# Pooling and convolution inputs of a two-layer encoder trunk: weights stationary, channels on the partitions, straight into the padded rows

## The chip, the cores and the metric

The kernel runs on one core of a Trainium2 chip. The metric is the device time of one execution in microseconds (us), here the median of three runs. The profile shows one further execution, recorded by the hardware profiler. Engines: PE is TensorE (PEld its weight load, which runs beside the matmuls), DVE is VectorE, ACT is ScalarE, POOL is GpSimd, SP is the queue that issues the DMAs of the weights.

## The reference, cut to what matters

The trunk has two layers over x of 256 tokens and 1024 channels, all in float32. Half of a layer:

```
h = rmsnorm(x, g_pre_mix)
(c_q, c_kv, k_r, p_in, s_u, s_v, cv_b, cv_c, cv_x, gate_logits) = split_cols(h @ w_in)
        # 256, 128, 32, 256, 256, 256, 256, 256, 256 and 4 x 1024 columns
y_a = mla_branch(c_q, c_kv, k_r, ...) @ w_br_a     # 8-head latent attention, rotary key
y_b = pool_branch(p_in, ...) @ w_br_b              # trailing-window means over 2, 4, 8, 16 tokens
y_c = sgu_branch(s_u, s_v, ...) @ w_br_c           # spatial gate within blocks of 128 tokens
y_d = (cv_b * conv3(cv_c * cv_x)) @ w_br_d         # causal 3-tap convolution along the tokens
merged = sum over branches of sigmoid(gate) * y
x = x + rmsnorm(merged @ w_out, g_post_mix)
```

The other half is a SwiGLU FFN of 2816 channels between two more norms. Pooling and convolution run along the tokens, so the kernel wants their inputs p_in, cv_b and cv_c * cv_x with channels on the partitions and tokens along the row.

## The kernel before

**Products.** Float32 products are made of float32r parts. Each operand is split into a high part and the rest: `mac` (L317, L318, L319) issues three matmuls, high x high, low x high, high x low. The activations of the first norm stand as `hh` (high) and `hl` (low), one pair of tiles for each half of 128 tokens (`hT_tiles`), channels on the partitions. The gain g is multiplied in there; the reciprocal root of each token (`rstd`, one number per token) is multiplied in later, on the product.

**Weights** come in pieces of 128 x 1024 (512 KB), in the order of a plan. The SP queue brings a piece into one of four staging buffers `st`; ACT copies it rounded into the high tile (L267), DVE subtracts to get the low one (L287); both are `u` tiles, of which there are 24. `pump` starts a piece, `settle` issues the DVE half, and the staging buffer is free when the DVE half is done. A piece of the projection has 2 of the 8 blocks k of 128 rows, and all columns of its group: `unit` runs the 2 x 3 matmuls of one piece for one half, and the four pieces of a group are added up in one bank of PSUM for each half.

**Groups of the combined projection.** A is c_q, c_kv, k_r (416 columns), S the spatial gate's (512), P is p_in with cv_b, the first 256 columns of the convolution (512), C the other two (512). After them come the four branches' gates (`group2`, evicted by a tanh on ACT), two groups of 512 columns each. In every one the activations of a half are the stationary side (128 x 128), the weights move, and the result has tokens on the partitions.

- `evict_p` (ACT, L931) and `evict_c` (ACT L935, DVE L936) multiply by `rstd`, C's second half with its first in one step.
- `g_misc`, once it starts, transposes these results: per half 2 transposes of the product cv_c * cv_x, and 4 of p_in and cv_b (L439, in `transposes`), copied by ACT (L789, L794, L795) into `zT`, `pT_` and `cT_`, rows of 16 zeros and 256 tokens. Then come the convolution (L804 on ACT, L805 to L807 on DVE), the pooling, the spatial gate.

**Order.** The order on each engine is written by hand. The main line issues the units; between them `tick()` advances the spawned generators, each with a delay in ticks, then issues the waiting DVE halves of conversions, and starts the next piece when few are ahead. An engine runs its instructions in the order in which they were issued. `att` is spawned ahead of the P group with a delay of 8 ticks: `g_proj` takes sums of squares on ACT, the rotary key (`rope`, DVE, L631 and on), the reciprocal root (`g_rsqrt`, DVE, L406 to L418, one Newton step per tick), the copies of the transposed key (L664), the transposes of c_q and c_kv with their split (`split_scaled`, ACT L446, DVE L447), and then the q products. A q product is 12 matmuls of 256 columns into one of the two `mm` banks, emptied on DVE by a multiply with the table of cosines (L685), so that the third product needs the bank that the first multiply has read. `misc` (`g_misc`) is spawned behind the C group with a delay of 3. The first piece of layer 0 is converted in the prologue, and the sums of squares for `rstd` there (`g_first`) run beside the A and S groups; `finish(first)` ends them within the P group, and `g_evict` then empties the A and S banks (L889, L895).

**The FFN** has a form of product that the change uses too. `block` (L1096, L1101) takes a piece with all 8 blocks k of 128 columns. The weights are stationary; the activations move, with the high and low parts of both halves beside each other in one row of 512: 8 matmuls of high weights x 512 columns, 8 of low weights x the 256 high columns. The result has channels on the partitions; its high and low sums are added up by `total` (ACT copy L1106, DVE add L1107, DVE multiply by a row L1108). That row, `rrow`, holds the reciprocal root of each token along the row on all partitions: `g_rrow` makes it with two copies on DVE (L1085), two transposes, and a copy on ACT.

Of the kernel before, what the change touches and what calls it, by code (L numbers as in the profile page):

```python
# [11 lines left out]
F32R = mybir.dt.float32r  # L12
# [31 lines left out]
EV = 2  # L44
# [151 lines left out]
def trunk(ctx: ExitStack, tc, x, xT, wall, small, const, qtab, gpost, out):  # L196
# [156 lines left out]

    def hT_tiles(h):
        return T([P, NK, P], f"hh{h}", 1, F32R), T([P, NK, P], f"hl{h}", 1, F32R)
# [253 lines left out]
    class Part:  # L609


        def __init__(self, tiles, s, h):
            self.tiles, self.s, self.h = tiles, s, h

        def __getitem__(self, at):
            k = at[1]
            return self.tiles[k // 2][:, k % 2, self.s, self.h * P:(self.h + 1) * P]

    for l in range(NL):
        sg = gains(l)  # L620
        a_sb, s_sb, p_sb, z_sb = [None, None], [None, None], [None, None], [None, None]
# [156 lines left out]
        def g_misc():  # L778
            L = PAD + SEQ
            zT = tok()[:, :].rearrange("p (c t) -> p c t", c=2)  # L780
            cT_ = tok()[:, :].rearrange("p (c t) -> p c t", c=2)
            pT_ = tok()[:, :].rearrange("p (c t) -> p c t", c=2)
            nc.gpsimd.memset(pT_[:, :, 0:PAD], 0.0)
            nc.gpsimd.memset(zT[:, :, 0:PAD], 0.0)
# [131 lines left out]
        else:  # L916
            o = {}
            for h, i in lead_order(8):
                if h == 1 and i == 0:
                    finish(turn)  # L920
                g, w, ev = (("A", 416, evict_a), ("S", 512, evict_s))[i // 4]
# [7 lines left out]
        def evict_p(h):  # L929
            p_sb[h] = tok()  # L930
            nc.scalar.activation(p_sb[h][:, :512], pp[h], AF.Identity, scale=rstd[h])  # L931

        def evict_c(h):
            z_sb[h] = tok()
            nc.scalar.activation(z_sb[h][:, :256], pc[h][:, 0:256], AF.Identity, scale=rstd[h])  # L935
            nc.vector.scalar_tensor_tensor(z_sb[h][:, 256:512], pc[h][:, 256:512], rstd[h], z_sb[h][:, 0:256],  # L936
                                           op0=ALU.mult, op1=ALU.mult)

# [3 lines left out]
        pp = [mm(), mm()] if l == 0 else [acc(), acc()]  # L942
        if l == 0:
# [8 lines left out]
            for n, (h, i) in enumerate(pairs(4)):  # L952
                unit(l, ("P",), i, h, hT, pp[h], 512)
                if n == EV:
                    finish(first)
                    late = spawn(g_evict())
                if i == 3:
                    if h == 0:
                        finish(late)
                    evict_p(h)  # L960
# [18 lines left out]
        def g_merged(h, q):  # L979
            if q == 0:  # L980
# [4 lines left out]
            split_scaled(hh[:, 4 * q:4 * q + 4, :].rearrange("p k t -> p (k t)"),  # L985
                         hl[:, 4 * q:4 * q + 4, :].rearrange("p k t -> p (k t)"), t, 0.5)
# [94 lines left out]
        def g_rrow():  # L1081

            rb = tok()
            for h in range(2):
                nc.vector.tensor_copy(rb[:, h * P:(h + 1) * P], rf[h].to_broadcast([P, P]))  # L1085
            yield RW
            t = tp()
            transposes(t, [rb[:, h * P:(h + 1) * P] for h in range(2)])
            nc.scalar.copy(rrow, t[:, :SEQ])

        def block(key):

            pc_ = W((l,) + key)
            o = mm()
            for k in range(NK):
                nc.tensor.matmul(o, pc_[0][:, k * P:(k + 1) * P], hx[k // 2][:, k % 2].rearrange("p s t -> p (s t)"),  # L1096
                                 start=(k == 0), stop=False)
                if k == 5:
                    tick()
            for k in range(NK):  # L1100
                nc.tensor.matmul(o[:, :SEQ], pc_[1][:, k * P:(k + 1) * P], hx[k // 2][:, k % 2, 0, :], start=False,  # L1101
                                 stop=(k == NK - 1))
            return o
# [39 lines left out]
        for h, u in lead_order(8):  # L1143
            if u == 0:
                finish(gturn[h])
                if h == 1:
                    rr = spawn(g_rrow(), 1)
# [81 lines left out]
```

## Time and profile before

| what | value |
|---|---|
| three runs | 803.78, 804.70, 804.86 us; median 804.7 |
| profiled execution | 803.72 us, of which its span is 801.9 |
| mean granted clock of TensorE | 0.997 |
| matmuls of `mac` with `hh` and `hl` (L317, L318, L319) | 424 of each, 399, 387 and 388 ns |
| conversions: ACT (L267), DVE (L287) | 268 of each, mean 1047 and 1215 ns |
| busiest of DVE's and ACT's groups | L287 with 318.8 us, L267 with 273.3 us |
| transfers | 148.11 MB, mean 185 GB/s |

The span is the time from the first recorded instruction to the last. Busy time of PE counts the matmuls as their ends are modelled; a matmul's own duration is longer than the distance from its start to the next one's, since they are pipelined. In rows of instructions the columns are the start in us, the duration, the engine, the line of the kernel, the operation, output <- inputs by the program's names with their partitions x elements, and how many stand in the row; in brackets follows the idle time of the engine ahead of it, and what it waited for. In rows of the chain they are the start, the duration, the engine, output and line.

### The profile page before, as it was taken

How to read it: one execution, taken by the hardware profiler on the slowest of the kernel's cores; microseconds unless marked ns; L12 is line 12 of the kernel's file. 1: busy time of each engine (PE TensorE's matmuls, PEld its weight loads, DVE VectorE, ACT ScalarE, POOL GpSimd, SP SyncE). 2: the span in 40 equal slices, each digit the busy share in tenths (PEclk: the TensorE clock that was granted, in tenths of full speed). 3: DMA queues.
4: the chain of work that ended last, by engine and by line, in shares of the span. 5: the costliest groups of instructions: out<-in, count | busy, mean ns of one | idle time of the engine just before them, and what ended most of it. 6: DMA issues, size and time to landing. Idle time of an engine off the chain costs nothing.

```text
span 801.9 us, 10903 instructions
## 1 busy us (share of the span) xinstructions
PE 791.0 (99%) x3982; PEld 664.2 (83%) x3982; DVE 598.5 (75%) x1094; ACT 452.8 (56%) x776; POOL 3.9 (0%) x16
## 2 busy tenths in 40 slices
PE   8999999999999999999999999999999999999996
PEld 7888887888888888888788888878888888888885
DVE  6687976748888777777885698764689787777773
ACT  6767655444665555555665675644357555555551
POOL 0000000000000000000000000000000000000000
PEclk9999999999999999999999999999999999999998
DMA  8866444455564555655655545355555555655631
GB/s 305 315 218 208 159 158 157 167 207 171 191 211 152 178 196 183 201 194 171 228 158 189 209 160 179 131 175 197 181 182 186 182 184 184 192 192 187 190 106 52
DMA packets 42245, 148.11 MB, mean 185 GB/s; under 512 B 4688, under 2 KB 5840, under 8 KB 42192
## 3 DMA queue, kind: packets, MB, share of 16 engines
q1 hardware_dynamic: 41328, 145.12, 54.1%
q0 software_dynamic: 576, 2.10, 0.7%
q8 instruction: 31, 0.51, 0.3%
q10 hardware_dynamic: 288, 0.21, 0.1%
q14 instruction: 22, 0.18, 0.1%
HBM read 146.36 MB, written 1.05 MB: 184 GB/s over the span
## 4 chain that ended last, share of the span: by engine, by line
PE 86%; DVE 7%; DMA 3%; ACT 2%; issue 1%; SPq 0%; DVEq 0%; ACTq 0%
PE acc L319 18%; PE acc L317 18%; PE acc L318 18%; PE mm L1096 14%; PE mm L1101 7%; DVE u L287 3%; PE tp L439 3%; DMA st<-wall 2%; PE mm L317 2%; PE mm L318 2%; PE mm L319 2%; PE mm L714 1%; DMA x<-x 1%; PE acc L742 1%; ACT u L267 1%
## 5 line engine op out<-in xcount | busy, mean ns | idle before, releaser
L287 DVE TENSOR_TENSOR u<-st,u 128x1024 fp32r<-128x1024 f32 (+1 forms) x268 | 318.8, 1215 | 51.9 <-ACT u L267 51.5
L267 ACT ACTIVATE u<-st 128x1024 fp32r<-128x1024 f32 (+1 forms) x268 | 273.3, 1047 | 19.1 <-DMA st<-wall 18.3
L317 PE MATMUL acc<-u,hh 128*128 128x512 f32 (+1 forms) x424 | 169.1, 399 | 0.0
L319 PE MATMUL acc<-u,hh 128*128 128x512 f32 (+1 forms) x424 | 164.7, 388 | 0.2 <-DVE u L287 0.2
L318 PE MATMUL acc<-u,hl 128*128 128x512 f32 (+1 forms) x424 | 164.3, 387 | 0.0
L1096 PE MATMUL mm<-u,u 128*128 128x512 f32 x576 | 144.4, 392 | 0.0
L1096 PEld LDWEIGHTS mm<-u,u 128*128 128x128 f32 x576 | 105.3, 188 | 20.8
L317 PE MATMUL acc<-u,s2k 128*128 128x512 f32 x256 | 101.2, 395 | 0.0
L319 PE MATMUL acc<-u,s2k 128*128 128x512 f32 x256 | 100.8, 394 | 0.3 <-DVE u L287 0.3
L318 PE MATMUL acc<-u,s2k 128*128 128x512 f32 x256 | 100.4, 392 | 0.0
L319 PEld LDWEIGHTS acc<-u,hh 128*128 128x128 f32 x424 | 79.6, 188 | 17.1 <-DVE u L287 0.8
L317 PEld LDWEIGHTS acc<-u,hh 128*128 128x128 f32 x424 | 79.8, 188 | 14.4 <-issue 0.3
L318 PEld LDWEIGHTS acc<-u,hl 128*128 128x128 f32 x424 | 79.8, 188 | 14.2
L1101 PEld LDWEIGHTS mm<-u,u 128*128 128x128 f32 x576 | 78.6, 190 | 5.6
L1101 PE MATMUL mm<-u,u 128*128 128x256 f32 x576 | 80.3, 282 | 0.0
L1024 ACT ACTIVATE gate<-acc,rhalf 128x512 f32<-128x512 f32 x32 | 22.1, 689 | 64.7 <-PE acc L319 64.6
L319 PEld LDWEIGHTS acc<-u,s2k 128*128 128x128 f32 x256 | 48.1, 188 | 11.1 <-DVE u L287 1.2
L317 PEld LDWEIGHTS acc<-u,s2k 128*128 128x128 f32 x256 | 48.2, 188 | 9.3 <-issue 0.3
L318 PEld LDWEIGHTS acc<-u,s2k 128*128 128x128 f32 x256 | 48.1, 188 | 9.1
L1107 DVE TENSOR_TENSOR tok<-mm,tok 128x256 f32<-128x256 f32 x72 | 30.3, 421 | 27.6 <-ACT tok L1106 27.4
L1106 ACT COPY tok<-mm 128x256 f32<-128x256 f32 x72 | 26.6, 370 | 42.6 <-PE mm L1101 39.6
L442 ACT ACTIVATE s2k<-tok 128x256 fp32r<-128x256 f32 (+1 forms) x38 | 16.3, 429 | 53.8 <-DVE tok L1121 53.8
(172 smaller groups left out, 747.1 us busy)
## 6 DMA issues: line engine op xcount, KB each, us to landing
st<-wall SPq DMA_DIRECT2D x261, 512.0 KB, 3.9
st<-wall SPq DMA_DIRECT2D x7, 416.0 KB, 3.9
gpost<-gpost POOLq DMA_DIRECT2D x4, 512.0 KB, 4.2
x<-x SPq DMA_DIRECT2D x2, 512.0 KB, 7.1
small<-small SPq DMA_DIRECT2D x2, 512.0 KB, 4.2
u<-xT SPq DMA_DIRECT2D x3, 256.0 KB, 6.1
st<-wall SPq DMA_DIRECT2D x2, 256.0 KB, 4.3
out<-x SPq DMA_DIRECT2D x2, 256.0 KB, 2.0
```

The source lines that it names most:

```text
L267: nc.scalar.activation(hi[:, :w], st[:, :w], AF.Copy)
L287: nc.vector.tensor_tensor(lo[:, :w], st[:, :w], hi.bitcast(F32)[:, :w], op=ALU.subtract)
L317: nc.tensor.matmul(out_, a[0][aw], w[0][ws], start=start, stop=False)
L318: nc.tensor.matmul(out_, a[1][aw], w[0][ws], start=False, stop=False)
L319: nc.tensor.matmul(out_, a[0][aw], w[1][ws], start=False, stop=stop)
L439: nc.tensor.transpose(dst[:, i * P:(i + 1) * P], s, ident)
L442: nc.scalar.activation(hi, src, AF.Copy)
L1024: nc.scalar.activation(gt[h], pgt[h], AF.Tanh, scale=rhalf[h])
L1096: nc.tensor.matmul(o, pc_[0][:, k * P:(k + 1) * P], hx[k // 2][:, k % 2].rearrange("p s t -> p (s t)"), start=(k == 0), stop=False)
L1101: nc.tensor.matmul(o[:, :SEQ], pc_[1][:, k * P:(k + 1) * P], hx[k // 2][:, k % 2, 0, :], start=False, stop=(k == NK - 1))
L1106: nc.scalar.copy(dst, o[:, SEQ:2 * SEQ])
L1107: nc.vector.tensor_tensor(dst, o[:, 0:SEQ], dst, op=ALU.add)
```

## The change

A piece of P or C now holds all 8 blocks k of one block of 128 columns (in `host_piece`, with `uses` 1), so four pieces make a group as before, with the same bytes. Each is one `block` of the form described for the FFN, its weights stationary, its result with channels on the partitions. `total` adds the two sums and multiplies by the row of reciprocal roots, writing straight into the padded rows `zcp`; the last two blocks of C are multiplied into the first two there. `evict_p`, `evict_c`, the twelve transposes per layer and their copies are gone. The row is made in the mixer's half of each layer too: its two transposes stand within the second P block of layer 0 (`mid`), and in `g_rrow`, spawned in the S group, in layer 1. To let one moving row hold high and low of both halves, the four tiles `hh`, `hl` become one tile `hx`, of which `Part` gives the pieces. `Part`, `block`, `total` and `g_rrow` are moved out to serve both uses, unchanged in what they issue for the FFN. `g_misc` starts with the convolution at once: its first four steps, a tick each, were the transposes.

```
 def uses(key):
-    if key[1] in ("wg", "wu"):
+    if key[1] in ("wg", "wu", "P", "C"):
         return 1
...
 def host_piece(inp, key):
+    if g in ("P", "C"):
+        c = [a + P * i for a, b in cols[g] for i in range((b - a) // P)][key[2]]
+        return kxn(inp["w_in"][l], 0, NK, [(c, c + P)])
...
     def hT_tiles(h):
-        return T([P, NK, P], f"hh{h}", 1, F32R), T([P, NK, P], f"hl{h}", 1, F32R)
+        if h == 0:
+            hx_now[0] = T([P, NK, 2, SEQ], "hx", 1, F32R)
+        return tuple(Part([hx_now[0]], s, h) for s in range(2))
...
+    def rows_in(rs):
+        rb = tok()
+        for h in range(2):
+            nc.vector.tensor_copy(rb[:, h * P:(h + 1) * P], rs[h].to_broadcast([P, P]))
+        return rb
+
+    def rows_out(rrow, rb):
+        t = tp()
+        transposes(t, [rb[:, h * P:(h + 1) * P] for h in range(2)])
+        nc.scalar.copy(rrow, t[:, :SEQ])
...
+    def block(key, o, both, high, mid=None):
+        pc_ = W(key)
+        for k in range(NK):
+            nc.tensor.matmul(o, pc_[0][:, k * P:(k + 1) * P], both(k), start=(k == 0), stop=False)
+            if k == 5:
+                if mid is not None:
+                    mid()
+                tick()
+        for k in range(NK):
+            nc.tensor.matmul(o[:, :SEQ], pc_[1][:, k * P:(k + 1) * P], high(k), start=False, stop=(k == NK - 1))
+        return o
+
+    def total(dst, o, tmp, rrow):
+        nc.scalar.copy(tmp, o[:, SEQ:2 * SEQ])
+        nc.vector.tensor_tensor(tmp, o[:, 0:SEQ], tmp, op=ALU.add)
+        nc.vector.tensor_tensor(dst, tmp, rrow, op=ALU.mult)
...
         def g_misc():
-            zT = tok()[:, :].rearrange("p (c t) -> p c t", c=2)
...
-            for h in range(2):
-                o = PAD + h * P
-                t = tp()
-                transposes(t, [z_sb[h][:, 256 + i * P:256 + (i + 1) * P] for i in range(2)])
-                nc.scalar.copy(zT[:, :, o:o + P], t[:, :256].rearrange("p (c t) -> p c t", c=2))
-                yield 1
-                t = tp()
-                transposes(t, [p_sb[h][:, i * P:(i + 1) * P] for i in range(4)])
-                t4 = t.rearrange("p (c t) -> p c t", c=4)
-                nc.scalar.copy(pT_[:, :, o:o + P], t4[:, 0:2, :])
-                nc.scalar.copy(cT_[:, :, o:o + P], t4[:, 2:4, :])
-                yield 1
+            zT, cT_, pT_ = zcp
...
+        zcp = [tok()[:, :].rearrange("p (c t) -> p c t", c=2) for _ in range(3)]
...
+        def evict_pc(g, i, o):
+            dst = zcp[(2 if i < 2 else 1) if g == "P" else 0][:, i % 2, PAD:PAD + SEQ]
+            v = tok()
+            if g == "C" and i >= 2:
+                total(v[:, 0:SEQ], o, v[:, 0:SEQ], row)
+                nc.vector.tensor_tensor(dst, dst, v[:, 0:SEQ], op=ALU.mult)
+            else:
+                total(dst, o, v[:, 0:SEQ], row)
...
         if l == 0:
...
+            for i in range(4):
+                o = block((l, "P", i), tp() if i == 2 else mm(), both, high, mid if i == 1 else None)
+                if i == 0:
                     finish(first)
+                    rb[0] = rows_in(rstd)
+                    first_o = o
+                else:
+                    if i == 1:
+                        evict_pc("P", 0, first_o)
+                        late = spawn(g_evict())
+                    evict_pc("P", i, o)
                 tick()
+            finish(late)
         else:
-            group2(l, ("P",), hT, pp, 512, evict_p)
-        pc = [acc(), acc()]
-        group2(l, ("C",), hT, pc, 512, evict_c)
+            for i in range(4):
+                o = block((l, "P", i), tp() if i == 2 else mm(), both, high)
+                finish(rr)
+                evict_pc("P", i, o)
+                tick()
+        for i in range(4):
+            evict_pc("C", i, block((l, "C", i), acc(), both, high))
+            tick()
```

In the changed kernel the lines have other numbers: L317 to L319 of before are L319 to L321 there, L439 is L458, L287 is L289, L664 is L709, L447 is L466, L685 is L730, L805 to L807 are L834 to L836; `block` is L649 and L655, `total` L660 to L662, the product of C's blocks L981.

PE in layer 0, the start of the P group, before: `mm_350` and `mm_351` are the banks of the two halves, `u` the high and low tiles of the first and the second weight piece, `hh` and `hl` the activations (4 and 5 of half 0, 6 and 7 of half 1).

```order
L317 MATMUL mm_350<-u_49_261,hh_4_72 128x512
L318 MATMUL mm_350<-u_49_261,hl_5_73 128x512
L319 MATMUL mm_350<-u_50_262,hh_4_72 128x512
L317 MATMUL mm_350<-u_54_283,hh_4_72 128x512
L318 MATMUL mm_350<-u_54_283,hl_5_73 128x512
L319 MATMUL mm_350<-u_55_284,hh_4_72 128x512
L317 MATMUL mm_351<-u_49_261,hh_6_74 128x512
```

The same place now, with the first two blocks; `hx` is the one tile of the activations, `tok_376` holds the copies of `rstd`.

```order
L649 MATMUL mm_353<-hx_72,u_46_258 128x512 x8
L655 MATMUL mm_353<-hx_72,u_47_259 128x256 x8
L649 MATMUL mm_385<-hx_72,u_51_280 128x512 x6
L458 MATMUL tp_392<-ident_69,tok_376 128x128 x2
L649 MATMUL mm_385<-hx_72,u_51_280 128x512 x2
L655 MATMUL mm_385<-hx_72,u_52_281 128x256 x8
```

Each piece is now used up by 16 matmuls in one bank, and the two transposes of the row stand behind the sixth matmul of the second block.

DVE in layer 1, from the last Newton step of the reciprocal root (`ry`) on, before: L664 copies the transposed key, L936 is the eviction of C's first half with its product, L447 the low part of the split of c_q and c_kv.

```order
L418 SCALAR_TENSOR_TENSOR ry_4223<-ra_4224,ry_4223 128x4
L664 COPY u_878_4279<-tp_4199 64x1024
L664 COPY u_879_4280<-tp_4199 64x1024
L936 SCALAR_TENSOR_TENSOR tok_4294<-acc_4214,ry_3879,tok_4294 128x256
L287 TENSOR_TENSOR u_882_4286<-st_4170,u_881_4285 128x1024
L447 SCALAR_TENSOR_TENSOR s2k_4311<-tp_4313,cst_70,s2k_4309 128x128 x2
L447 SCALAR_TENSOR_TENSOR s2k_4312<-tp_4313,cst_70,s2k_4310 128x128
```

The same stretch now, from the same step on: L661, L662 and L981 are the add, the multiply by the row and the product of the third C block.

```order
L437 SCALAR_TENSOR_TENSOR ry_4302<-ra_4303,ry_4302 128x4
L289 TENSOR_TENSOR u_886_4343<-st_4223,u_885_4342 128x1024
L709 COPY u_889_4376<-tp_4278 64x1024
L709 COPY u_890_4377<-tp_4278 64x1024
L661 TENSOR_TENSOR tok_4395<-acc_4363,tok_4395 128x256
L662 TENSOR_TENSOR tok_4395<-tok_4395,rrow_3952 128x256
L981 TENSOR_TENSOR tok_4157<-tok_4157,tok_4395 128x256
L289 TENSOR_TENSOR u_893_4383<-st_4250,u_892_4382 128x1024
L466 SCALAR_TENSOR_TENSOR s2k_4410<-tp_4412,cst_70,s2k_4408 128x128 x2
L466 SCALAR_TENSOR_TENSOR s2k_4411<-tp_4412,cst_70,s2k_4409 128x128
```

Where one operation emptied C's half there are three for a block, and a conversion stands ahead of the copies of the key.

DVE in layer 1, from the halving of `rstd` (L973) to the first multiply by the table (`tab`), before:

```order
L973 TENSOR_SCALAR rhalf_4346<-ry_3879 128x1
L973 TENSOR_SCALAR rhalf_4347<-ry_4023 128x1
L287 TENSOR_TENSOR u_904_4365<-st_4243,u_903_4364 128x1024
L287 TENSOR_TENSOR u_907_4377<-st_4283,u_906_4376 128x1024
L685 TENSOR_TENSOR u_912_4401<-mm_4403,tab_111 128x512
L685 TENSOR_TENSOR u_912_4401<-mm_4435,tab_111 128x512
```

And now, where L834 to L836 are the convolution (two taps for each half of the channels, and the product with cv_b):

```order
L1028 TENSOR_SCALAR rhalf_4456<-ry_3918 128x1
L1028 TENSOR_SCALAR rhalf_4457<-ry_4061 128x1
L289 TENSOR_TENSOR u_916_4475<-st_4340,u_915_4474 128x1024
L834 SCALAR_TENSOR_TENSOR tok_4497<-tok_4157,cst_70,tok_4497 128x256
L835 SCALAR_TENSOR_TENSOR tok_4497<-tok_4157,cst_70,tok_4497 128x256
...
L836 TENSOR_TENSOR tok_4497<-tok_4497,tok_4158 128x2x256
L289 TENSOR_TENSOR u_919_4487<-st_4380,u_918_4486 128x1024
L730 TENSOR_TENSOR u_923_4512<-mm_4514,tab_108 128x512
L730 TENSOR_TENSOR u_923_4512<-mm_4539,tab_108 128x512
```

The five operations of the convolution have come ahead of the first two multiplies by the table.

More of the change, by code (lines that the diff above doesn't have):

```diff
@@ L43 @@
 NW = 7
-EV = 2
 XAT, XD = (8, 9), 8
@@ L916, in trunk @@
         else:
+            row1 = T([P, SEQ], "rrow", 1)
             o = {}
@@ L920, in trunk @@
                     finish(turn)
+                    rr = spawn(g_rrow(row1, rstd), 1)
                 g, w, ev = (("A", 416, evict_a), ("S", 512, evict_s))[i // 4]
@@ L927, in trunk @@
                 tick()
[L929 to L937, printed above, removed]
         if l == 0:
@@ L941, in trunk, with both, high @@
         att = spawn(g_att(), AS)
-        pp = [mm(), mm()] if l == 0 else [acc(), acc()]
+        zcp = [tok()[:, :].rearrange("p (c t) -> p c t", c=2) for _ in range(3)]
+        for i in (0, 2):
+            nc.gpsimd.memset(zcp[i][:, :, 0:PAD], 0.0)
+        row = T([P, SEQ], "rrow", 1) if l == 0 else row1
+        htile = hx_now[0]
+        def both(k):
+            return htile[:, k].rearrange("p s t -> p (s t)")
+        def high(k):
+            return htile[:, k, 0, :]
+        def evict_pc(g, i, o):
[6 more added lines that the diff above has]
+                total(dst, o, v[:, 0:SEQ], row)
         if l == 0:
@@ L950, in g_evict, with mid @@
                     yield 1
-            for n, (h, i) in enumerate(pairs(4)):
-                unit(l, ("P",), i, h, hT, pp[h], 512)
-                if n == EV:
-                    finish(first)
[L956 to L960, printed above, removed]
+            rb = [None]
+            def mid():
+                rows_out(row, rb[0])
+            for i in range(4):
+                o = block((l, "P", i), tp() if i == 2 else mm(), both, high, mid if i == 1 else None)
+                if i == 0:
+                    finish(first)
+                    rb[0] = rows_in(rstd)
[5 more added lines that the diff above has]
+                    evict_pc("P", i, o)
                 tick()
+            finish(late)
         else:
-            group2(l, ("P",), hT, pp, 512, evict_p)
-        pc = [acc(), acc()]
-        group2(l, ("C",), hT, pc, 512, evict_c)
+            for i in range(4):
[6 more added lines that the diff above has]
+            tick()
         sm = small_load(l)
@@ L1079, in trunk @@
         rrow = T([P, SEQ], "rrow", 1)
[L1081 to L1103, printed above, removed]
-        def total(dst, o):
-            nc.scalar.copy(dst, o[:, SEQ:2 * SEQ])
-            nc.vector.tensor_tensor(dst, o[:, 0:SEQ], dst, op=ALU.add)
-            nc.vector.tensor_tensor(dst, dst, rrow, op=ALU.mult)
         def gate_up(b):
@@ L1112, in gate_up @@
             gv, uv = v[:, 0:SEQ], v[:, SEQ:2 * SEQ]
-            o = block(("wg", b))
+            o = block((l, "wg", b), mm(), both, high)
             if b == B0:
                 finish(rr)
-            total(gv, o)
+            total(gv, o, gv, rrow)
             nc.scalar.activation(sg_[:, :SEQ], gv, AF.Sigmoid)
@@ L1119, in gate_up @@
             tick()
-            total(uv, block(("wu", b)))
+            total(uv, block((l, "wu", b), mm(), both, high), uv, rrow)
             nc.vector.tensor_tensor(gv, gv, uv, op=ALU.mult)
@@ L1139, in down, with both, high @@
                         start=(b == 0), stop=(b == NB - 1))
+        def both(k):
+            return hx[k // 2][:, k % 2].rearrange("p s t -> p (s t)")
+        def high(k):
+            return hx[k // 2][:, k % 2, 0, :]
         gact = [None, None]
@@ L1146, in trunk @@
                 if h == 1:
-                    rr = spawn(g_rrow(), 1)
+                    rr = spawn(g_rrow(rrow, rf), 1)
             g, i = u // 4, u % 4
```

29 lines of the change are left out of this document (16 added, 13 removed).

## The prediction

> **What bounds the kernel now.** I read the page first, then who waited on TensorE (PE), then the instructions of each engine in order of time. The page gives the span, the busy times and the engines' shares of the chain that ended last:
>
> ```profile
> span 801.9 us, 10903 instructions
> PE 791.0 (99%) x3982; PEld 664.2 (83%) x3982; DVE 598.5 (75%) x1094; ACT 452.8 (56%) x776; POOL 3.9 (0%) x16
> PE 86%; DVE 7%; DMA 3%; ACT 2%; issue 1%; SPq 0%; DVEq 0%; ACTq 0%
> ```
>
> PE is the bound: 99% busy, 86% of the chain. VectorE (DVE) is next, and 75% is an average. Idle time of DVE costs nothing only as long as nothing that PE waits for stands late in DVE's queue. So the change has two accounts: what it adds to PE's own work, and whether DVE still delivers in time in the two stretches (one per layer) in which it adds DVE work. Lines are those of before.
>
> **PE's own work.** The P and C groups are now 12 three-matmul products per piece. The P group of layer 0 starts at the first row, the C group at the second; two blocks of the form that the change uses stand in the chain of waits, in the FFN; then one group of 2 and one of 4 transposes of the pooling and convolution inputs, each with the start of the second matmul behind it:
>
> ```profile
> 26.12 0.39 PE L317 MATMUL mm<-u,hh 128*128 128x512 f32 x1
> 37.00 0.39 PE L317 MATMUL acc<-u,hh 128*128 128x512 f32 x1
> ...
> 243.75 1.84 PE mm L1096 x8
> 245.60 0.95 PE mm L1101 x8
> 246.55 1.84 PE mm L1096 x8
> ...
> 60.27 0.38 PE L439 MATMUL tp<-ident,tok 128*128 128x128 f32 x2
> 60.72 0.39 PE L318 MATMUL acc<-u,hl 128*128 128x512 f32 x1
> 63.29 0.60 PE L439 MATMUL tp<-ident,tok 128*128 128x128 f32 x4
> 63.96 0.40 PE L318 MATMUL acc<-u,hl 128*128 128x512 f32 x1
> ```
>
> A group takes 37.00 - 26.12 = 10.88 us for 48 matmuls, 0.227 each. A block takes 246.55 - 243.75 = 2.80, four of them 11.20: +0.32 a group, four groups +1.28. Two transposes cost 0.45 - 0.227 = 0.22 us, four 0.67 - 0.227 = 0.44. Removed are two of each per layer, 1.32, in both layers 2.64. Added is one pair per layer that turns rstd into a row, 0.44. PE's own work: 1.28 + 0.44 - 2.64 = **-0.92 us**. A rule of the Trainium skill weighs against that row: "TensorE: Matmul & The Clock Gate", Back-to-back issue gap, gives N/2.4 + 2.5 ns, 216 for 512 columns and 109 for 256, so a block would cost as much as the work it replaces (2.60 against 2.59) and PE's own sum would be about -2.0. The trace has 0.227 and 2.80, and I keep those.
>
> **ScalarE (ACT)** loses evictions and copies and gains one 0.37 us copy per block. At 56% it is not on the path by its load, but DVE waits for it at one place below.
>
> **DVE's work.** Each block is now read by an ACT copy, an add and a multiply. The nearest rows are the same three operations in the FFN; the row copies have theirs too (minimum, median, maximum):
>
> ```profile
> 365.96 0.37 ACT L1106 COPY tok<-mm 128x256 f32<-128x256 f32 x1
> 366.41 0.42 DVE L1107 TENSOR_TENSOR tok<-mm,tok 128x256 f32<-128x256 f32 x1
> ...
> 341.43 0.42 DVE L1107 TENSOR_TENSOR tok<-mm,tok 128x256 f32<-128x256 f32 x1
> 341.88 0.42 DVE L1108 TENSOR_TENSOR tok<-tok,rrow 128x256 f32<-128x256 f32 x1
> 342.34 0.43 DVE L1121 TENSOR_TENSOR tok<-tok 128x256 f32<-128x256 f32 x1
> ...
> L1085 DVE COPY tok<-ry x4: 218/222/222, 229.5 to 624.3; 128x128 f32<-128x128 f32 x4
> ```
>
> The add starts 0.45 after the copy, and dependent operations start 0.455 apart: 0.91 a block, 1.37 for the last two C blocks with their product. Per layer 6 x 0.91 + 2 x 1.37 + 2 x 0.22 = 8.6 us come in; two products of 256 columns (L936) go, 0.8 at the 0.42 of their like. So DVE gets 7.8 us more per layer. Where does it stand? Behind the P group comes the attention's serial part (rope, reciprocal root, copies of kT, split of c_q) with weight conversions (L287) between, up to L685, which empties the first `mm` bank of the q projection. There are two such banks, so PE's third q product must wait for the first L685. Layer 1 before, DVE in order of time, each row the first of its step:
>
> ```profile
> 423.67 3.50 DVE L287 TENSOR_TENSOR u<-st,u 128x1024 fp32r<-128x1024 f32 x3 [3.46 <-ACT u L267]
> 431.83 1.22 DVE L287 TENSOR_TENSOR u<-st,u 128x1024 fp32r<-128x1024 f32 x1 [4.66 <-ACT u L267]
> 432.98 0.28 DVE L631 TENSOR_TENSOR tok<-u,cst 128x32 f32<-128x32 f32 x2
> 435.41 0.17 DVE L406 TENSOR_SCALAR rv<-ms 128x4 f32<-128x4 f32 x1 [0.78 <-ACT junk L429]
> 436.39 1.23 DVE L287 TENSOR_TENSOR u<-st,u 128x1024 fp32r<-128x1024 f32 x1
> 437.53 0.16 DVE L416 TENSOR_TENSOR ra<-ry 128x4 f32<-128x4 f32 x1
> 438.03 1.23 DVE L287 TENSOR_TENSOR u<-st,u 128x1024 fp32r<-128x1024 f32 x1
> 439.91 2.46 DVE L664 COPY u<-tp 64x1024 f32<-64x1024 f32 x2 [0.19 <-PE tp L439]
> 444.13 0.34 DVE L447 SCALAR_TENSOR_TENSOR s2k<-tp,cst,s2k 128x128 fp32r<-128x128 f32 x1
> 445.96 1.22 DVE L287 TENSOR_TENSOR u<-st,u 128x1024 fp32r<-128x1024 f32 x1
> 449.32 0.21 DVE L973 TENSOR_SCALAR rhalf<-ry 128x1 f32<-128x1 f32 x2
> 452.28 0.69 DVE L685 TENSOR_TENSOR u<-mm,tab 128x512 f32<-128x512 f32 x1
> 461.93 0.48 DVE L805 SCALAR_TENSOR_TENSOR tok<-tok,cst,tok 128x256 f32<-128x256 f32 x1
> 464.49 3.49 DVE L287 TENSOR_TENSOR u<-st,u 128x1024 fp32r<-128x1024 f32 x3
> ```
>
> From the end of P to the end of the first L685 DVE takes 452.97 - 432.98 = 20.0 us, with 0.78 and 0.19 of idle in these rows. In the new order the same stretch holds more, and since the convolution no longer waits for four ticks of transposes, its five operations (L805 to L807) stand ahead of the first L685, with a conversion. The new stretch, from the add of the fourth P block: three totals 2.73, two totals with product 2.74, rope 1.65 (432.98 to 435.41 less its 0.78 of idle), seven conversions at 1.14 (436.39 to 437.53) 7.98, reciprocal root 0.98 (435.41 to 436.39) and two more steps of 0.50 (437.53 to 438.03), kT copies 2.46, two splits at 1.83 (444.13 to 445.96) 3.66, rhalf 0.21, convolution 2.56 (461.93 to 464.49), L685 0.69; and one wait of 0.95 (estimate: a conversion on ACT at 0.97 and a copy at 0.37, less 0.4 that DVE still works), because the copy of the fourth C block stands on ACT behind the first split and a conversion. Sum **27.6 us**.
>
> PE needs for the same stretch, from the end of the fourth P block to the third q product: four blocks 11.2, two kr transposes 0.22, two groups of three 0.66 (between the two prices above), four gate units of six matmuls 5.44, and q product, unit, q product, unit 1.42 + 1.36 + 1.42 + 1.36 (a q product is 12 matmuls of 256 columns at 0.95/8): **23.1**. DVE starts some 0.6 after PE, so PE has to stop, in all 5.1 us, first at the gate weights' second piece and the first q product, and last at the third.
>
> In layer 1 the rows are these: PE's last P matmul, and its third q product; for layer 0 the third q product, and ACT from its last early DMA wait on.
>
> ```profile
> 432.46 0.39 PE L319 MATMUL acc<-u,hh 128*128 128x512 f32 x1
> 456.48 0.28 PE L317 MATMUL mm<-s2k,u 128*128 128x256 f32 x1
> ...
> 61.88 0.28 PE L317 MATMUL mm<-s2k,u 128*128 128x256 f32 x1
> ...
> 33.06 1.06 ACT L267 ACTIVATE u<-st 128x1024 fp32r<-128x1024 f32 x1 [0.92 <-DMA st<-wall]
> 34.03 0.60 ACT L889 ACTIVATE u<-acc,ry 128x416 f32<-128x416 f32 x1
> 34.52 1.05 ACT L267 ACTIVATE u<-st 128x1024 fp32r<-128x1024 f32 x1
> ```
>
> Layer 1: P ends at 432.7; with +0.32 and the row transposes 0.22 at 433.2; the add follows at 433.85, and the first L685 ends at 461.45 where the third q product began at 456.48: +5.0, and the four transposes still ahead there are gone, -0.44: **+4.5**. Layer 0: ACT frees itself from its DMA wait at 33.06 and has then, ahead of the copy of the fourth P block, four conversions at 0.97 (with that one, 33.06 to 34.03), two L889 at 0.49 (34.03 to 34.52), two L895 at 0.6 (estimate: 512 columns against L889's 416), the row copy and three block copies at 0.3 (estimate: 0.37, and the next starts a little before the end): 33.06 + 7.3 = 40.35. The add stands at 40.8, the first L685 ends at 68.4, against 61.88: +6.5, less 0.44: **+6.1**. A first stop, for the row's transposes in the second block, is part of that and not added. PE is the bound everywhere behind, with no idle time to give back. Behind the third q product DVE has no more work than before, and PE is later by the stops, so DVE catches up.
>
> **Bounds.** No wait is shared twice: the stops add up to the lateness at the last one. From below the DVE sum could be 1.5 us less a layer (ACT's copy earlier, conversions moved), from above 2 more (more hand-overs between ACT and DVE like the one I count). The new waits are queued on PE itself, and nothing else waits for PE there but DVE and ACT. The SP queue issues the same pieces; its buffers come free up to 2 us later, while the pieces lie ready before their use by more than that.
>
> **Sum.** -0.92 of PE's own work is in both figures. 6.1 + 4.5 = +10.6 us on the profiled execution, whose own time is 803.72 us (span 801.9, 1.8 around it): 814.3. It lies 1.0 under the median of the three runs, 804.7: **815 us**.
>
> **Rivals.**
> 1. DVE's additions lie in its idle time (25% of the span, and 3.46 and 4.66 us in front of two rows above), and only PE's account counts: 804.7 - 0.9 = 803.8, not slower. It decides if the first L685 ends before 61.9 and 456.5. Against it: the additions stand behind PE's P group, after those gaps, in a stretch that shows 0.78 and 0.19 of idle. A rule of the Trainium skill speaks for it: "Perfetto Trace Analysis", Identifying the Most-Contended Engine, would have the engine with the highest occupancy decide, here PE with 99% against 75%; the rows agree for the span as a whole. Chance 0.12.
> 2. One layer's stretch only: layer 0 late, layer 1 covered (it gives -0.5): 804.7 + 6.1 - 0.5 = 810.3. For it: layer 1's queues are less full at the start of P. Chance 0.12.
> 3. One tile makes half 0's matmuls wait until half 1's activations are written:
>
> ```profile
> 400.81 0.35 PE L317 MATMUL acc<-u,hh 128*128 128x416 f32 x1
> 411.21 1.12 DVE L519 SCALAR_TENSOR_TENSOR hl<-tp,cst,hh 128x128 fp32r<-128x128 f32 x4
> ```
>
> In layer 1 half 0 begins at 400.8, half 1 is written until 412.3: up to 11.5 us more, 826. Against it: the built program's waits there go by the parts of the tile that are written. Chance 0.03.
> 4. More hand-overs than I counted, in both layers: 820 and above. Chance 0.07.
>
> **How the numbers follow.** My case has 0.66, at 811 to 819; with rival 2 it makes 0.78, and the range 808 to 819 takes these in with some of the rest. 0.2% is 1.6 us, about what a measurement of this kernel can tell from no change: faster than 803.1 has 0.04 (rival 1 with before's own small stops gone), within it 0.08, slower 0.88.
>
> **What would show it.** PE waiting on DVE in two stretches, some 6 us in layer 0 and 5 in layer 1, the last of it for the multiply by the table; DVE without idle from 41 to 68 and from 434 to 461; no wait of half 0's matmuls for half 1's writes; blocks of 2.80. If PE shows no such waits, DVE's account is wrong; if it waits and the total is under 808, PE made time good behind it.

## The result, and the profile after

The changed kernel takes 813.5 us (median of 5 runs, 813.26 to 814.13) against 804.7; the ratio estimated from all runs is 1.0113, with a 95% interval of 1.0102 to 1.0124. The profiled execution took 813.26, its span 811.5, 9.6 more than before. First the page of the changed kernel, its span, busy times and shares of the chain that ended last:

```profile
span 811.5 us, 11030 instructions
PE 793.0 (98%) x4026; PEld 665.5 (82%) x4026; DVE 610.9 (75%) x1130; ACT 450.6 (56%) x774; POOL 3.9 (0%) x16
PE 77%; DVE 12%; ACT 4%; DMA 4%; issue 1%; DVEq 0%; SPq 0%; ACTq 0%
```

DVE has 12.4 us more work and the same 75%, yet its share of the chain went from 7% to 12%, ACT's from 2% to 4%, and PE's from 86% to 77%. Who PE waited for tells where (in all, times, longest):

```profile
PE mm L319 <- DVE u L730: 3.2, 2, 1.6
PE tp L458 <- DVE u L709: 1.8, 2, 1.1
PE acc L321 <- DVE rhalf L1028: 0.7, 2, 0.4
PE mm L649 <- DVE tok L661: 0.7, 1, 0.7
PE mm L890 <- DVE tok L882: 0.5, 1, 0.5
```

The largest is the q product that needs the bank which the multiply by the table (L730) reads, once a layer; then the transposes of c_q and c_kv, whose bank of PSUM the copies of the key (L709) still hold. Both are of one kind: PE waits for a bank that DVE has not yet read. The third q product of layer 0 and of layer 1:

```profile
67.54 0.39 PE L319 MATMUL mm<-s2k,u 128*128 128x256 f32 x1 [1.61 <-DVE u L730]
...
466.10 0.39 PE L319 MATMUL mm<-s2k,u 128*128 128x256 f32 x1 [1.56 <-DVE u L730]
```

DVE in layer 1, in order of time, with the rows between left out: the fourth P block's add, the steps named in the prediction, the first multiplies by the table:

```profile
439.29 0.42 DVE L661 TENSOR_TENSOR tok<-mm,tok 128x256 f32<-128x256 f32 x1 [0.77 <-ACT tok L660]
...
440.09 0.29 DVE L676 TENSOR_TENSOR tok<-u,cst 128x32 f32<-128x32 f32 x2
...
448.65 2.46 DVE L709 COPY u<-tp 64x1024 f32<-64x1024 f32 x2
...
456.18 0.42 DVE L661 TENSOR_TENSOR tok<-acc,tok 128x256 f32<-128x256 f32 x1 [0.86 <-ACT tok L660]
...
461.67 0.48 DVE L834 SCALAR_TENSOR_TENSOR tok<-tok,cst,tok 128x256 f32<-128x256 f32 x1
...
464.23 1.22 DVE L289 TENSOR_TENSOR u<-st,u 128x1024 fp32r<-128x1024 f32 x1
465.36 1.28 DVE L730 TENSOR_TENSOR u<-mm,tab 128x512 f32<-128x512 f32 x2
```

From the fourth add to the end of the first L730 (465.36 + 0.69) DVE takes 26.8 us, against 20.0 before. In layer 0 the same stretch goes from 40.74 to 67.49:

```profile
40.74 0.42 DVE L661 TENSOR_TENSOR tok<-mm,tok 128x256 f32<-128x256 f32 x1
...
66.80 1.28 DVE L730 TENSOR_TENSOR u<-mm,tab 128x512 f32<-128x512 f32 x2
```

The chain of waits over 440 to 468 us, the stretch of layer 1, holds hardly any PE:

```profile
by line: DVE u L289 29.0%; DVE u L709 8.7%; DVE tok L662 7.7%; issue 5.6%; ACT s2k L465 5.3%; DVE tok L661 5.2%; DVE s2k L466 4.7%; DVE tok L835 3.5%; ACT u L269 3.4%; DVE tok L981 3.0%; DVE tok L834 2.9%; PE mm L319 2.6%; DVE u L730 2.2%; 
```

How late PE is can be read at work that both kernels do. The last gate evictions of layer 0 and of layer 1, before and then after:

```profile
178.78 0.69 ACT L1024 ACTIVATE gate<-acc,rhalf 128x512 f32<-128x512 f32 x1 [1.08 <-PE acc L319]
573.47 0.69 ACT L1024 ACTIVATE gate<-acc,rhalf 128x512 f32<-128x512 f32 x1 [1.08 <-PE acc L319]
```

```profile
183.93 0.69 ACT L1078 ACTIVATE gate<-acc,rhalf 128x512 f32<-128x512 f32 x1 [1.08 <-PE acc L321]
...
583.30 0.69 ACT L1078 ACTIVATE gate<-acc,rhalf 128x512 f32<-128x512 f32 x1 [1.08 <-PE acc L321]
```

Layer 0 brings +5.15 (its first P matmul starts 0.33 later than before, 26.45 for 26.12), layer 1 another 9.83 - 5.15 = +4.68; of the 9.83 the rest of the program gives 0.2 back.

### The profile page after: what moved, and what is told of

It reads as the page before. It is cut to its first block, busy times and chain, and to the rows that moved or that the text cites. A ratio compares the mean times of both kernels' runs of the same rounds, so it can differ in the third digit from the quotient of the medians.

```text
span 811.5 us, 11030 instructions
## 1 busy us (share of the span) xinstructions
PE 793.0 (98%) x4026; PEld 665.5 (82%) x4026; DVE 610.9 (75%) x1130; ACT 450.6 (56%) x774; POOL 3.9 (0%) x16
## 4 chain that ended last, share of the span: by engine, by line
PE 77%; DVE 12%; ACT 4%; DMA 4%; issue 1%; DVEq 0%; SPq 0%; ACTq 0%
PE acc L319 15%; PE acc L321 15%; PE acc L320 15%; PE mm L649 15%; PE mm L655 8%; DVE u L289 5%; DMA st<-wall 3%; PE tp L458 2%; ACT u L269 2%; PE mm L319 1%; PE mm L321 1%; PE mm L320 1%; DVE tok L662 1%; PE mm L759 1%; DVE tok L661 1%
## 5 line engine op out<-in xcount | busy, mean ns | idle before, releaser
L289 DVE TENSOR_TENSOR u<-st,u 128x1024 fp32r<-128x1024 f32 (+1 forms) x268 | 318.9, 1214 | 40.1 <-ACT u L269 39.8
L319 PE MATMUL acc<-u,hx 128*128 128x512 f32 (+1 forms) x376 | 150.2, 400 | 0.0
L321 PE MATMUL acc<-u,hx 128*128 128x512 f32 (+1 forms) x376 | 146.3, 389 | 0.9 <-DVE rhalf L1028 0.7
L320 PE MATMUL acc<-u,hx 128*128 128x512 f32 (+1 forms) x376 | 145.5, 387 | 0.0
L649 PE MATMUL mm<-u,u 128*128 128x512 f32 x576 | 144.4, 392 | 0.0
L649 PEld LDWEIGHTS mm<-u,u 128*128 128x128 f32 x576 | 105.3, 188 | 20.9
L321 PE MATMUL acc<-u,s2k 128*128 128x512 f32 x256 | 100.7, 393 | 0.2 <-DVE u L289 0.2
L319 PE MATMUL acc<-u,s2k 128*128 128x512 f32 x256 | 100.7, 393 | 0.0
L321 PEld LDWEIGHTS acc<-u,hx 128*128 128x128 f32 x376 | 70.6, 188 | 17.0 <-DVE u L289 2.8
L655 PEld LDWEIGHTS mm<-u,u 128*128 128x128 f32 x576 | 78.6, 190 | 5.6
L320 PEld LDWEIGHTS acc<-u,hx 128*128 128x128 f32 x376 | 70.8, 188 | 12.5
L319 PEld LDWEIGHTS acc<-u,hx 128*128 128x128 f32 x376 | 70.6, 188 | 12.6 <-issue 0.3
L655 PE MATMUL mm<-u,u 128*128 128x256 f32 x576 | 80.3, 282 | 0.0
L661 DVE TENSOR_TENSOR tok<-mm,tok 128x256 f32<-128x256 f32 x78 | 32.8, 420 | 36.2 <-ACT tok L660 35.9
L321 PEld LDWEIGHTS acc<-u,s2k 128*128 128x128 f32 x256 | 48.1, 188 | 10.9 <-DVE u L289 0.9
L319 PEld LDWEIGHTS acc<-u,s2k 128*128 128x128 f32 x256 | 48.2, 188 | 9.4 <-issue 0.3
L660 ACT COPY tok<-mm 128x256 f32<-128x256 f32 x78 | 28.8, 370 | 46.6 <-PE mm L655 43.6
```

The costliest lines, as they stand in the source:

```text
L289: nc.vector.tensor_tensor(lo[:, :w], st[:, :w], hi.bitcast(F32)[:, :w], op=ALU.subtract)
L319: nc.tensor.matmul(out_, a[0][aw], w[0][ws], start=start, stop=False)
L320: nc.tensor.matmul(out_, a[1][aw], w[0][ws], start=False, stop=False)
L321: nc.tensor.matmul(out_, a[0][aw], w[1][ws], start=False, stop=stop)
L649: nc.tensor.matmul(o, pc_[0][:, k * P:(k + 1) * P], both(k), start=(k == 0), stop=False)
L660: nc.scalar.copy(tmp, o[:, SEQ:2 * SEQ])
```

## The experiments

Times are medians of the runs beside runs of the kernel before, on the same chip (804.46, 804.69 and 804.53 in the three groups). Lateness by layer is read at the same gate evictions, in the one profiled execution of each kernel. These differ by up to 1.9 us in when the first P matmul starts (26.1 to 28.0 us). Both forms show such a spread, 26.1 to 27.4 where P is made as before and 26.4 to 28.0 where it is made of blocks, so layer 0 is read with that in mind.

**Convolution late.** The convolution back behind the multiplies.

```
-        misc = spawn(g_misc(), MS)
+        misc = spawn(g_misc(), MS + 4)
```

> The changed kernel with one number altered: the misc generator starts 4 ticks later, so the convolution's five DVE operations stand behind all four multiplies by the table again, as before the change. Theory (DVE's serial stretch from the fourth P block to the first multiply by the table is longer than PE's, 26.7 against 23.1 us): the first multiply comes 2.56 us earlier in each layer, so the stop at the third q product (1.77 and 1.73 us beyond the normal distance) goes, the stops ahead of it stay: 813.5 - 3.5 = 810.0 (809 to 811). Rival, the convolution's place is the whole loss: about 804. Rival, the loss is the block form itself and its hand-overs to ACT: 813.5, unchanged.

Measured: 810.33 (ratio 1.0066, 1.0054 to 1.0079), 3.2 less than the changed kernel. Of the larger waits, that for L730 is gone, and with it the 0.5 us of the spatial gate's matmuls (L890); these stay:

```profile
PE tp L458 <- DVE u L709: 1.8, 2, 1.1
...
PE mm L649 <- DVE tok L661: 0.8, 1, 0.8
PE acc L321 <- DVE rhalf L1028: 0.7, 2, 0.4
```

So a third of the loss came from work that the change does not even add, but lets run earlier. The edit delays all of `g_misc`, of which the five operations of the convolution stand in the stretch; the lateness that layer 1 adds falls from 4.68 to 1.95. The rival that the place is all of the loss falls.

**No totals.** P and C blocks emptied by one ACT copy; the low sums, the multiplies and the product are left out.

```
-            v = tok()
-            if g == "C" and i >= 2:
-                total(...)
...
+            nc.scalar.copy(dst, o[:, SEQ:2 * SEQ])
```

> The changed kernel, in which each P and C block is emptied by its ACT copy alone (left out: the low sums, the multiply by the row and the product of C's blocks, so all of their DVE work, 8.2 us a layer). PE runs the same blocks. Theory: DVE's stretch falls by 2.4 + 2.5 us and the wait of 0.85, from 26.7 to about 21, under PE's 23.1; all stops but the row's transposes in layer 0 (0.5) go, and PE's own account of -0.9 is what is left: 804.3 (803.5 to 805.5). Rival, block form on PE or the one tile costs the time: 812 to 813.5.

Measured: 804.47 (0.9995, 0.9987 to 1.0004). PE still runs every block, from one tile, and the convolution is still early; with the DVE work gone the loss is gone. Of the waits listed for the changed kernel two small ones are left, and layer 0 keeps a stop for the fourth block's bank, now for ACT:

```profile
PE mm L649 <- ACT tok L978: 1.1, 1, 1.1
...
PE mm L890 <- DVE tok L882: 0.5, 1, 0.5
PE mm L319 <- DVE u L730: 0.2, 1, 0.2
```

**One more multiply** behind each total, its result not used.

```
+            nc.vector.tensor_tensor(v[:, SEQ:2 * SEQ], v[:, 0:SEQ], row, op=ALU.mult)
```

> The changed kernel with one more DVE multiply (256 columns, result not used) behind each of the 8 totals of a layer. Theory: 5 of the 8 stand within the stretch that bounds, at 0.34 to 0.45 each 1.7 to 2.2 us in layer 1, and in layer 0 two or three more, because the early totals there run back to back: 2 to 3.2. Sum +4 to +5.4: 818 (817 to 819.5). Rival, DVE has idle time for it or ACT's hand-overs bound: 813.5 to 814.5.

Measured: 817.17 (1.0153, 1.0139 to 1.0167), +3.7: just under the theory's range of +4 to +5.4 as a difference, within its range as a time. The sixteen multiplies, of 0.34 to 0.42 us each, came out as 3.7 us, a little less than the expectation counts for those within the stretches; DVE's idle time, a quarter of the span, does not cover these.

**The kernel before, with DVE work added.**

```
+    def extra():
+        d = T([P, SEQ], "rrow", 1)
+        nc.vector.tensor_tensor(d, xs[:, 0, 0:SEQ], xs[:, 0, 0:SEQ], op=ALU.add)
+        nc.vector.tensor_tensor(d, d, xs[:, 0, 0:SEQ], op=ALU.mult)
...  # after every second unit of P and C: extra()
```

> The kernel before with 16 added DVE operations per layer (an add and a multiply of 256 columns behind every second unit of P and C, results not used), nothing else changed: DVE gets about as much work as the change adds, at the same places, without blocks, hand-overs to ACT or the convolution's new place. Theory: five pairs of 0.79 stand in the stretch, 3.95 us, of which about 0.8 fills idle time; layer 1 had 3.5 us of slack between the first multiply by the table (ends 452.97) and the third q product (456.48), layer 0 1.7 (60.2 and 61.88): no loss in layer 1, +1.5 in layer 0: 806.2 (805 to 808), so that DVE's load alone, without the convolution moved ahead and the hand-overs, is the smaller part. Rival, every microsecond of DVE's work there delays PE by one: 804.7 + 12.6 = 817. Rival, DVE's load is nothing and the block form is all: 804.7.

Measured: 809.05 (1.0049, 1.0035 to 1.0062), 2.85 above the expectation and outside its range. Lateness: 4.14 in layer 0 (the first P matmul starts 0.57 later than before), 1.27 in layer 1. The direction holds, the size does not, and the waits say why:

```profile
PE acc L319 <- DVE u L287: 2.3, 5, 1.3
...
PE tp L439 <- ACT u L664: 0.9, 1, 0.9
```

(L664 is the scaling of c_q on ACT in that kernel, which waits for DVE's reciprocal root.) I had counted only the way to the first multiply by the table. In the form before, a piece of weights is needed whole, its low half included, for the third matmul already, so DVE's delay meets PE earlier, at a conversion. DVE's load alone, without blocks, costs about half of what the change does.

**Sum on PE.** 24 matmuls of 256 columns into one sum, so that one DVE multiply empties a block (two for the last C blocks).

```
+    def block3(key, o, low, high, mid=None):
+        for k in range(NK):
+            for j, x_ in enumerate((high, low)):
+                nc.tensor.matmul(o[:, :SEQ], pc_[0][...], x_(k), start=(k == 0 and j == 0), stop=False)
...
+        for k in range(NK):
+            nc.tensor.matmul(o[:, :SEQ], pc_[1][...], high(k), start=False, stop=(k == NK - 1))
...
+                nc.vector.tensor_tensor(dst, o[:, 0:SEQ], row, op=ALU.mult)
```

> The changed kernel with the low sum added on PE: a P or C block is 24 matmuls of 256 columns into one bank (high weights x high, high weights x low, low weights x high), so a block is emptied by one DVE multiply (two for the last C blocks), without ACT copy and add. Theory: the DVE stretch falls from 26.7 by 1.1 (three totals of 0.79 to about 0.43) + 0.9 (two of 1.24 to 0.8) + 0.85 (no hand-over) to 23.9 us, PE's grows by 5 x 0.05 to 23.4: stops of 0.5 to 1 us a layer are left, and 16 blocks cost PE 0.7 more: 806 (804.8 to 807.5). Rival, the block form and one tile cost the time, whatever DVE does: 813 or more.

Measured: 806.21 (1.0018, 1.0010 to 1.0027). The stops for the multiply by the table (L744 in that kernel) are 0.36 and 0.37 us, in place of 1.61 and 1.56:

```profile
63.29 0.38 PE L319 MATMUL mm<-s2k,u 128*128 128x256 f32 x1 [0.36 <-DVE u L744]
...
459.06 0.38 PE L319 MATMUL mm<-s2k,u 128*128 128x256 f32 x1 [0.37 <-DVE u L744]
```

**Sum on PE and convolution late.** Both edits.

> The same with the convolution 4 ticks later, as before the change. Theory: DVE's stretch is 21.3 us against PE's 23.4, no stop is left but the early ones of layer 0 (about 0.5), and PE's own account is -0.9 + 0.7: 804.7 (804.0 to 805.7), no different from the kernel before. Rival: gains of the two edits do not add (e1 and e5 removed the same stops): 806.

Measured: 804.41 (0.9997, 0.9988 to 1.0006): as before, 9.1 us under the changed kernel. The gains add for the most part: 3.2 and 7.3 apart, 9.1 together, and not the 806 of the rival. The chain of waits over 430 to 470 us, the whole of this kernel's stretch in layer 1, is PE's again:

```profile
by line: PE acc L663 19.2%; PE acc L319 12.5%; PE acc L321 12.5%; PE acc L320 12.5%; PE acc L669 9.6%; PE mm L319 7.1%; PE mm L320 7.0%; PE mm L321 7.0%; PE mm L663 4.8%; PE tp L669 2.4%; PE mm L669 2.4%; PE tp L458 2.2%; PE tp L663 1.2%
```

**Multiplies on GpSimd**, with the convolution late.

```
+            nc.scalar.copy(v[:, 0:SEQ], o[:, SEQ:2 * SEQ])
+            nc.vector.tensor_tensor(v[:, 0:SEQ], o[:, 0:SEQ], v[:, 0:SEQ], op=ALU.add)
...
-                total(dst, o, v[:, 0:SEQ], row)
+                nc.gpsimd.tensor_tensor(dst, v[:, 0:SEQ], row, op=ALU.mult)
```

> The changed kernel with the convolution 4 ticks later and the multiplies by the row, and the two products of C, on GpSimd; ACT copies and DVE adds stay. Theory: DVE's stretch is 26.7 - 2.56 - 1.1 - 1.7 = 21.3 us against 23.1, no stop but the early ones: 804.6 - 0.9 + 0.5 = 804.2 (803.5 to 805.5). No trace here has a GpSimd multiply; what it takes only matters where the convolution waits for it. Rival, GpSimd and DVE slow each other, or the convolution's late rows stop the branch d product: 806 or more.

Measured: 807.0 (1.0029, 1.0018 to 1.0039), the rival's time. The engines slow each other. GpSimd's multiplies in layer 1, and below them DVE's rows, a conversion beside the first of these multiplies and a small operation at 441.8 beside the last:

```profile
435.05 1.66 POOL L985 TENSOR_TENSOR tok<-tok,rrow 128x256 f32<-128x256 f32 x1 [1.14 <-DVE tok L980]
437.85 0.74 POOL L985 TENSOR_TENSOR tok<-tok,rrow 128x256 f32<-128x256 f32 x1 [1.14 <-DVE tok L980]
441.81 0.74 POOL L985 TENSOR_TENSOR tok<-tok,rrow 128x256 f32<-128x256 f32 x1 [3.21 <-DVE ra L435]
```

```profile
434.89 1.22 DVE L289 TENSOR_TENSOR u<-st,u 128x1024 fp32r<-128x1024 f32 x1
437.35 0.42 DVE L980 TENSOR_TENSOR tok<-mm,tok 128x256 f32<-128x256 f32 x1 [1.24 <-ACT tok L979]
...
441.64 0.15 DVE L435 TENSOR_TENSOR ra<-ry 128x4 f32<-128x4 f32 x1
441.83 0.74 DVE L436 TENSOR_TENSOR ra<-ra,rv 128x4 f32<-128x4 f32 x1
442.60 0.16 DVE L437 SCALAR_TENSOR_TENSOR ry<-ra,ry 128x4 f32<-128x4 f32 x1
...
446.90 2.46 DVE L709 COPY u<-tp 64x1024 f32<-64x1024 f32 x2
```

A multiply on GpSimd takes 0.74, or 1.66 when a conversion runs on DVE beside it; and a DVE operation of 4 columns, 0.16 elsewhere, takes the whole 0.74 beside one on GpSimd. Each layer's rope and reciprocal root have three DVE operations so lengthened (by 1.6 us in all), and they stand ahead of the key copies: from the fourth block's add to these copies DVE takes 437.35 to 446.90, 9.55 us, where the changed kernel took 9.36 (439.29 to 448.65) with the multiplies still on DVE. So the stop for the bank that the copies hold stays as it was:

```profile
PE tp L458 <- DVE u L709: 2.0, 2, 1.1
```

The sum over the whole stretch did not show this: DVE is through with the first L730 after 22.5 us (437.35 to 459.89), under the 23.1 that the prediction counts for PE, and nothing waits for it there. PE met DVE at an earlier point.

**One tile in the kernel before.**

```
-        return T([P, NK, P], f"hh{h}", 1, F32R), T([P, NK, P], f"hl{h}", 1, F32R)
+        if h == 0:
+            hx_now[0] = T([P, NK, 2, SEQ], "hx", 1, F32R)
+        return tuple(hx_now[0][:, :, s, h * P:(h + 1) * P] for s in range(2))
```

> The kernel before with its four activation tiles made one, as the change has it, and nothing else. Theory: it costs nothing, since waits go by the parts written: 804.5 (within 1.2 us). Rival, half 0's matmuls wait for half 1's writes in layer 1: up to +11.5, 816.

Measured: 804.64 (0.9998, 0.9990 to 1.0007). The one tile costs nothing.

**Key copies on ACT**, convolution late.

```
-                nc.vector.tensor_copy(kT[e][rows], ...)
+                nc.scalar.copy(kT[e][rows], ...)
```

> The changed kernel with the convolution 4 ticks later (as e1) and the two copies of the transposed key on ACT in place of DVE (2.46 us a layer off DVE's stretch; the operations on DVE that the change added stay as they are). Theory: the stretch is 26.7 - 2.56 - 2.46 = 21.7 us against PE's 23.1, so the stops that e1 kept (for the key's bank 1.30 and 0.80, the q products 0.57 each, the gate 0.54 each) go, 4.3 in all, and the early ones of layer 0 (1.0) stay: 805.5 to 806 (804.5 to 807). Rival, what the change added costs by itself, wherever the stretch is relieved: 810.

Measured: 812.54 (1.0101, 1.0087 to 1.0116), 2.2 slower than without the move and far above the expectation. ACT and DVE in layer 1:

```profile
446.97 0.51 ACT L702 ACTIVATE u<-u,ry 128x256 f32<-128x256 f32 x1 [2.66 <-DVE ry L437]
448.48 2.03 ACT L709 COPY u<-tp 64x1024 f32<-64x1024 f32 x2
450.41 1.06 ACT L269 ACTIVATE u<-st 128x1024 fp32r<-128x1024 f32 x1
451.37 0.35 ACT L660 COPY tok<-acc 128x256 f32<-128x256 f32 x1
```

```profile
451.75 0.42 DVE L661 TENSOR_TENSOR tok<-acc,tok 128x256 f32<-128x256 f32 x1 [3.68 <-ACT tok L660]
```

DVE's work fell by 2.46, but the next block's total needs an ACT copy, and that now stands behind scaling, key copies and a conversion, all of which ACT can begin only when DVE has the reciprocal root: DVE idles 3.68 us. PE meets the delay at the conversions for the gates:

```profile
PE acc L321 <- DVE u L289: 3.2, 4, 1.3
```

In the kernel before the same move shows no gain either:

> The kernel before with the two copies of the transposed key on ACT, nothing else. Theory: there DVE's stretch (20.0 us) is under PE's already, so relieving it by 2.46 us gives nothing: 804.5 (within 0.2%). Rival, the copies cost PE time in any case: 802 or less.

Measured: 806.27 (1.0026, 1.0017 to 1.0035), a small loss of 1.7 us, just outside the 0.2% around 804.5. So the stretch is not a sum over DVE alone: it is one chain through DVE and ACT, whose links on ACT were covered by DVE work as long as they were short.

**Row transposes a block later in layer 0** (`mid` in the third P block, the first two blocks emptied behind it), on top of the key copies on ACT, and on top of the sum on PE.

```
-  o = block((l, "P", i), ..., mid if i == 1 else None)
+  o = block((l, "P", i), ..., mid if i == 2 else None)
```

> The same as e9, and in layer 0 the two transposes of the row stand within the third P block in place of the second, the first two blocks being emptied after it. Theory: the stops ahead of the fourth block (up to 0.5 at the transposes, 0.8 to 1.0 for its bank) come from ACT and DVE being late at the start; later transposes take away the first, but not the second, which waits for the first block's total, now later by a block: within 0.5 of e9, and a gain only if the transposes' stop was the larger.

Measured: 814.53 (1.0128, 1.0106 to 1.0151; runs from 812.5 to 818.3). That is 2.0 above e9 and outside the 0.5 forecast, but the runs spread over 5.8 us and the two intervals overlap; the profiled execution, 812.57, is 1.0 above that of e9 (811.55). The stop for the fourth block's bank is 2.3 us in its profile. The profile of e9 shows neither this stop nor one for the transposes, so there was nothing to win; how large the loss is isn't settled.

> e6 (sums on PE, convolution late) with the row's transposes in the third P block of layer 0. Theory: the only stop beyond 0.5 us that e6 shows and the kernel before does not is the one for these transposes (1.30); a block later it is gone: 804.4 - 1.0 = 803.4 (802.9 to 804.4), with PE's own account (-0.2) a little under the kernel before. Rival, the start of layer 0 is bound by ACT and the transfers, so that the stop only moves to the fourth block's bank: 804.4.

Measured: 805.82 (1.0017, 1.0005 to 1.0028), 1.4 above the same kernel with the earlier place. Its profile shows no stop for the transposes, and still layer 0 is 1.0 late, its first P matmul starting at 28.0. Of the eight profiles with the transposes in the second block, the stop that the move was to remove shows only in the two whose P group started early, at 26.4 (1.1 us in e6, 0.3 in the changed kernel), and in none that started at 27.1 or later: a later start takes its place. That points to the rival, a start bound by ACT and transfers, without showing it, and where the 1.4 us are isn't settled.

No version beat the kernel before.

## Why the prediction was right, point by point

- **Time and sign.** 815 forecast, 813.5 measured, inside the likeliest case's 811 to 819. Rivals 1 (covered by idle time) and 2 (one layer only) fall by the lateness: both layers pay, 5.15 and 4.68, where 6.1 and 4.5 were forecast. Rival 3 (waits between halves) falls by the one-tile kernel, rival 4 (820 and above) by the time. For rival 1 the prediction set PE's 99% against DVE's 75%; the page of the Trainium skill that it names judges TensorE by its weight loads and not by its matmul time; they are 83% here (PEld) and rank PE first just the same. No share of the whole span shows the stretch.
- **The mechanism** is shown, not only argued: taking the DVE work away (e2) removes the loss with every block left in place; adding to it (e3) adds to the time; moving it out of the stretch (e1) or doing it on PE (e5, e6) gives it back in about the amounts that the stretch predicts. What the sum up to the multiply by the table does not tell is whether PE meets DVE earlier: e4 and e7 were forecast too low for that reason. e9 was for another: the sum lacked a hand-over that the move to ACT made long, and the stretch of layer 1 took 25.5 us (438.76 to 464.24) where 21.7 were forecast.
- **DVE's sum** was 27.6, measured 26.8 in both layers. The mis-sized term is the totals: an operation that does not need the one before starts 0.34 behind it (439.75 to 440.09), so a total costs 0.80 (439.29 to 440.09) where I took 0.91 throughout, and one with product 1.24 for 1.37: 3 x 0.11 + 2 x 0.13 = 0.6 of the 0.8. The hand-over estimated at 0.95 is 0.86 in the row.
- **Layer 0** was put 0.9 us too late by this sum alone: the fourth add came at 40.74, as forecast (40.8), and L730 ended at 67.49 for 68.4.
- **Layer 1** is close (4.68 for 4.5) because two errors cancel. Less the 5.15 that it inherits, the first L730 ended at 460.9 for 461.45 (the sum 0.8 shorter, the fourth add 0.3 later than forecast). Against that, PE stops once more behind the third q product, where the prediction had DVE catch up: the spatial gate's matmuls (L890) wait 0.5 for DVE (L882) in layer 1. It is not the added work that makes this stop: e2, without the totals, has it, and of the kernels with blocks all have it in which `g_misc` starts at once (the changed one, e2, e3, e5) and none in which it starts four ticks later. The place that the change gives to `g_misc` was overlooked beyond the convolution.
- **PE's own work.** Blocks came 2.79 apart, as from the FFN's 2.80:

```profile
430.31 2.00 PE L649 MATMUL mm<-hx,u 128*128 128x512 f32 x8
432.15 1.11 PE L655 MATMUL mm<-hx,u 128*128 128x256 f32 x8
433.10 2.00 PE L649 MATMUL tp<-hx,u 128*128 128x512 f32 x8
```

  The estimate of 2.60, worked out from a formula of the Trainium skill ("TensorE: Matmul & The Clock Gate", Back-to-back issue gap), is not reached here either, and the measurement decides; the section gives that formula for an isolated matmul, and these stand in a stream. The 0.9 us that PE's account promised do not show in the time: with the DVE work away, e2 takes 804.47 beside 804.46 for the kernel before. Its profile still has 1.8 us of stops that the kernel before lacks (1.1, 0.5 and 0.2), which may hide them.
- **The places of the stops** were only half right. The last, for the multiply by the table, is there, and the largest. The first ones I put at the gate's second weight piece and the first q product; the larger early stop is at the second group of three transposes, for the bank that the key copies hold (1.14 in layer 0). I had followed weights and `mm` banks, and not the two `tp` banks. The total was not touched, since the stops add up to the lateness at the last one.
- **Not said:** that a third of the loss could be had back by four ticks of delay. The term was in the sum (2.56 for the convolution), and it was the cheapest of all to take out.

## What to carry to other kernels

An engine at 75% can bound: add up what stands between two points where the full engine hands work over and gets it back, and compare that with what the full engine has in between. Do so for every such pair of points, not only for the last. A change of operand order that saves transposes also moves work between engines; count the emptying of the banks, not only the products. Work that became ready earlier should not run earlier than what the bound engine waits for. And in a chain that passes between two engines, moving a link to the idler one can lengthen it.

## What the runs showed of the hardware

In e7 DVE and GpSimd did not run freely side by side on SBUF operands: a DVE operation of 128x4 took 0.74 us, and not 0.16, beside a GpSimd multiply of 0.74, and that multiply took 1.66 beside a DVE conversion of 1.22. A block of 24 matmuls of 256 columns costs PE 2.88 (from one block's start to the next in the chain of e6), against 2.79 for 8 of 512 and 8 of 256; for 16 blocks that is 1.4 us, where e5's expectation took 0.7:

```profile
431.41 1.92 PE mm L663 x16
...
434.29 1.92 PE acc L663 x16
```
